# The opening of a two-layer diffusion backbone in two-chunk steps, with the context moved between latent features and their products

## The chip, the cores and the metric

One core of a Trainium2 chip runs the whole program. The metric is the device time of one execution in microseconds (us), the median of several.

## What is computed

The input is a latent stream `x` and a context stream `ctx`, each 256 tokens of 1024 features, and two conditioning vectors. Each of two layers mixes tokens by four branches and then applies a feed-forward block. The change concerns only the start of layer 0, up to the products q, k and v of the first branch:

```
mod = silu(c) @ w_mod[0] + b_mod[0]        # same with c_ctx for the context
sh1, sc1, ... = split(mod, 6)
h_lat = rmsnorm(x, norm_g[0, 0]) * (1 + sc1) + sh1
h_ctx = rmsnorm(ctx, norm_g[0, 0]) * (1 + csc1) + csh1
q, k, v = (h @ w_in[0])[..., :256], [256:512], [512:768]     # both streams
q, k = rope(q * 0.125), rope(k)            # the latent ones only
```

Everything else of `h @ w_in[0]`, the branches, the output projection, the feed-forward block and layer 1 follows and is the same code before and after.

## The kernel before

**Layout.** Features lie on partitions: a hidden state is 8 chunks of 128 features by 512 tokens (256 latent, then 256 context), kept as a hi and a lo tile in fp32r (`h0hi`, `h0lo`). Weights come as blocks of 128x1024 float32 (0.5 MB), by SP's queue, into four raw buffers (two tags of two). A block for a product is split into a hi tile (ACT, L102) and a lo tile (DVE, L112); a product is three matmuls, hi x hi, hi x lo, lo x hi (`mm3`, L205). A block of conditioning weights is used raw, as it lands.

**Who sets the order.** The program is a list of `Step`s, written out by hand in `begin` (L1288) for the opening. Ahead of each step `Weights.pump` (L114) loads as many of the opening's blocks as find a raw buffer whose former block is split (or, for conditioning, used), and splits what the step needs; then the step's code is issued. Each engine works its own instructions in that order, and SP issues its loads in that order, waiting for the buffer of each.

**The opening.** `x` is loaded, its squares are summed on ACT (`square`), the inverse root of the mean comes from POOL, DVE scales it (`x_norm`, L1301), PE turns it so that features lie on partitions (`x_turn`, tile `x0t`), DVE copies it to `x0s`. Meanwhile the conditioning product runs: one block is one chunk of 128 input features by 1024 outputs, shift and scale of four of the eight chunks of features, and `mod_mm` (L256) multiplies it in two matmuls of 512 columns. Its two results go to two strips of 32 of the array's columns (the two streams' conditioning vectors are the 32-column stationary operand `cs`). After eight blocks, a half, ACT copies the result to `modrows` (L1342), PE turns it (`modt`, L278), DVE adds the biases and makes `am` and `sh` (L283 to L286). Then `modulate` (L451) makes the hidden features of the half: `hf = x * am + sh`, one chunk on DVE and one on ACT, hi on ACT (L466), lo on DVE (L449).

The first half's products follow: v for two token tiles, then k, q, for the latent stream, with `v_part` (L1058) and `qk_part` (L1067), four chunks each, into banks of PSUM that `clear` (L1039) has filled with zeros. The eight blocks of the second conditioning half are multiplied between the products of the first half, with the context's features and products in between. Then the second half is turned to features (`late`, L1379), and its products follow, v of the latent stream first. After the context's v the values are centred on DVE (L678, L679); after k and q `rotate` (L714) applies the rope table, on ACT and DVE. The rope table and other constants are loaded by `fixed` (L649). The opening ends with the first matmul of the gate projection (`gps`); `retention` (L747) then starts beside it, its first products being `ktp` and, from `kt` and `vd`, `st` (L775).

Of the kernel before, what the change touches and what calls it, by code (L numbers as in the profile page):

```python
# [17 lines left out]
P = 128  # L18
# [14 lines left out]
MOD_ORDER = (0, 2, 1, 3)  # L33
# [4 lines left out]
WARM = (3,)  # L38
# [22 lines left out]
class Weights:  # L61
# [76 lines left out]

    def split_to(self, nth):
# [17 lines left out]
def kernel(ctx: ExitStack, tc: tile.TileContext, a: dict, out: bass.AP):  # L157
# [46 lines left out]

    def mm3(ps, st, mv, first, last):  # L205
# [38 lines left out]
    chan = load(cst, [P, DEPTH, 2, 4], a["chan"], "chan", nc.scalar)  # L244
    bsel = load(cst, [P, 2], a["c_bsel"], "bsel", nc.scalar)
    e12 = load(dec, [P, 2, 2 * PIECE], a["c_e12"], "e12", nc.scalar)
    kexp = load(dec, [P, 2, 2], a["c_kexp"], "kexp", nc.scalar)
# [8 lines left out]
    def mod_mm(k, half, raw):  # L256
        if "ps" not in mods:
            mods["ps"] = bank("m", "modps")
        ps = mods["ps"]
        for j in range(2):  # L260
            q = 2 * half + j
            nc.tensor.matmul(
                ps[32 * q : 32 * q + 32, :],
                lhsT=cs[:, k, :],
                rhs=raw[:, j * 512 : (j + 1) * 512],
                start=(k == 0),
                stop=(k == KC - 1),
            )
# [4 lines left out]
    def mod_cols(half, tiles, rows):  # L273

        pt = bank("b", f"modt{half}", [4, 64])
        hs = slice(64 * half, 64 * half + 64)
        for cb in range(4):
            nc.tensor.transpose(pt[:, cb, :], rows[hs, cb * P : (cb + 1) * P], ident[hs, hs])  # L278
        am, sh = tiles
        ks = slice(4 * half, 4 * half + 4)  # L280
        for s in range(2):
            b = [bcol[:, 0, kind, ks] for kind in range(2)]
            nc.vector.tensor_tensor(sh[:, s, ks], pt[:, :, s], b[0], op=ALU.add)  # L283
            nc.vector.tensor_tensor(am[:, s, ks], pt[:, :, 32 + s], b[1], op=ALU.add)
            nc.vector.scalar_tensor_tensor(
                am[:, s, ks], am[:, s, ks], 1.0, gcol[:, 0, 0, ks], op0=ALU.add, op1=ALU.mult  # L286
            )
# [325 lines left out]
    def mixer(l, h, hnext, start=None):  # L613
# [422 lines left out]
        if l == 0:  # L1036
            vps, kps, qps = {}, {}, {}

            def clear():  # L1039
# [4 lines left out]
                yield  # L1044
                for i in range(2):
                    vps[i], kps[i] = bank("a", f"vps{i}", [2, MIX]), bank("a", f"kps{i}")
                for n in (0, *WARM):
                    for i in range(2):
                        for ps in (vps[i].rearrange("p a b -> p (a b)"), kps[i]):
# [516 lines left out]
```

## Time and profile before

| | |
|---|---|
| time, median of 3 runs | 1244.37 us (1244.19 to 1245.08) |
| time of the profiled execution | 1246.01 us |
| its span, first to last instruction | 1244.2 us |
| PE busy | 1205.8 us, 97% of the span |
| DVE busy | 776.5 us, 62% |
| ACT busy | 452.4 us, 36% |
| POOL busy | 41.2 us, 3% |
| moved by DMA | 206.29 MB, mean 166 GB/s |
| chain of work that ended last, share of PE | 89% |

PE is the tensor engine, DVE the vector engine, ACT the scalar engine, POOL the general one; SP issues loads. Busy times are sums over instructions; a busy PE is not PE at its peak, since matmuls are pipelined and each record is longer than its share of the pace. Start times count from the first instruction of the span.

### The profile page before, as it was taken

Reading aid. Unit: us, or ns where it says so; the run is one execution under the profiler, and the core shown is the slowest. Engines: PE = TensorE matmul, PEld = TensorE weight load, DVE = VectorE, ACT = ScalarE, POOL = GpSimd, SP = SyncE. Lnnn points to the kernel's source line nnn. Section 1 sums busy time; section 2 is a strip of 40 time slices with the busy share of each in tenths; the row PEclk is TensorE's granted clock in tenths of the full one; section 3 lists DMA queues with packets and bytes.
Section 4 is the critical chain, followed back from the end, with each engine's and each line's share of the span. In section 5 each row is a group of like instructions: output and inputs, shape, how many; then the busy total and the mean of one; then the engine's idle time right before and its main releaser. Section 6 shows DMA issues by size and latency. Waiting matters only on the chain.

```text
span 1244.2 us, 17237 instructions
## 1 busy us (share of the span) xinstructions
PE 1205.8 (97%) x6790; PEld 1032.6 (83%) x6790; DVE 776.5 (62%) x1242; ACT 452.4 (36%) x712; POOL 41.2 (3%) x39
## 2 busy tenths in 40 slices
PE   6999999999999989999999999989999999999997
PEld 2687878888888788888888888779889998999986
DVE  4454464477887465776777674475666666666644
ACT  3332332323322453222222222354335445444532
POOL 1500000000000000000000000000000000000000
PEclk9999999999999989999999999999999999999999
DMA  8542323546755224666756783343455563656662
GB/s 291 180 130 84 102 85 107 209 151 168 203 176 190 82 94 126 225 209 158 246 185 205 226 270 105 112 134 136 123 153 183 178 225 116 201 176 185 196 220 88
DMA packets 66433, 206.29 MB, mean 166 GB/s; under 512 B 14640, under 2 KB 18224, under 8 KB 66352
## 3 DMA queue, kind: packets, MB, share of 16 engines
q1 hardware_dynamic: 65200, 204.96, 52.8%
q8 instruction: 53, 0.87, 0.3%
q10 hardware_dynamic: 1152, 0.24, 0.1%
q14 instruction: 28, 0.23, 0.1%
HBM read 204.06 MB, written 1.11 MB: 165 GB/s over the span
## 4 chain that ended last, share of the span: by engine, by line
PE 89%; DVE 4%; ACT 3%; issue 1%; DMA 1%; POOL 0%; SPq 0%; DVEq 0%; POOLq 0%; ACTq 0%
PE up L208 10%; PE up L209 10%; PE up L207 10%; PE gate L207 7%; PE gate L209 7%; PE gate L208 7%; PE dn L209 4%; PE dn L208 4%; PE dn L207 4%; PE pb L209 2%; PE pb L207 2%; PE pb L208 2%; PE wo L209 1%; PE wo L207 1%; PE wo L208 1%
## 5 line engine op out<-in xcount | busy, mean ns | idle before, releaser
L317 DVE SCALAR_TENSOR_TENSOR mjunk<-raw_mod,crow 128x1024 bf16<-128x1024 f32 x128 | 156.4, 1222 | 11.1 <-DMA raw_mod<-in_w_modt 8.9
L208 PE MATMUL up<-hm0lo,hi_up 128*128 128x512 f32 (+1 forms) x384 | 143.6, 374 | 0.5 <-DVE hm0lo L449 0.5
L207 PE MATMUL up<-hm0hi,hi_up 128*128 128x512 f32 (+1 forms) x384 | 143.8, 375 | 0.0
L209 PE MATMUL up<-hm0hi,lo_up 128*128 128x512 f32 (+1 forms) x384 | 143.7, 374 | 0.0
L112 DVE TENSOR_TENSOR lo_up<-raw_up,hi_up 128x1024 fp32r<-128x1024 f32 x88 | 107.5, 1223 | 36.2 <-ACT hi_up L102 36.2
L112 DVE TENSOR_TENSOR lo_gt<-raw_gt,hi_gt 128x1280 fp32r<-128x1280 f32 x64 | 95.3, 1489 | 30.5 <-ACT hi_gt L102 30.2
L207 PE MATMUL gate<-h0hi,hi_gt 128*128 128x512 f32 x256 | 100.5, 392 | 0.0
L207 PE MATMUL up<-hm1hi,hi_up 128*128 128x256 f32 x352 | 100.3, 285 | 0.0
L208 PE MATMUL up<-hm1lo,hi_up 128*128 128x256 f32 x352 | 100.3, 285 | 0.0
L209 PE MATMUL up<-hm1hi,lo_up 128*128 128x256 f32 x352 | 100.1, 284 | 0.0
L209 PE MATMUL gate<-h0hi,lo_gt 128*128 128x512 f32 x256 | 99.6, 389 | 0.0
L208 PE MATMUL gate<-h0lo,hi_gt 128*128 128x512 f32 x256 | 99.6, 389 | 0.0
L102 ACT ACTIVATE hi_up<-raw_up 128x1024 fp32r<-128x1024 f32 x88 | 92.1, 1048 | 7.2 <-DMA raw_up<-in_w_up 6.6
L102 ACT ACTIVATE hi_gt<-raw_gt 128x1280 fp32r<-128x1280 f32 x64 | 81.0, 1266 | 28.0 <-DMA raw_gt<-in_w_gate 28.0
L112 DVE TENSOR_TENSOR lo_dn<-raw_dn,hi_dn 128x1024 fp32r<-128x1024 f32 x44 | 53.6, 1224 | 51.4 <-ACT hi_dn L102 51.2
L988 ACT ACTIVATE sg<-gate 128x512 f32<-128x512 f32 (+1 forms) x64 | 31.3, 490 | 148.1 <-PE gate L209 146.8
L208 PEld LDWEIGHTS up<-hm0lo,hi_up 128*128 128x128 f32 x384 | 73.4, 191 | 13.1 <-DVE hm0lo L449 0.7
L207 PEld LDWEIGHTS up<-hm0hi,hi_up 128*128 128x128 f32 x384 | 73.5, 191 | 12.6
L209 PEld LDWEIGHTS up<-hm0hi,lo_up 128*128 128x128 f32 x384 | 73.3, 191 | 12.4
L102 ACT ACTIVATE hi_dn<-raw_dn 128x1024 fp32r<-128x1024 f32 x44 | 46.4, 1058 | 91.8 <-PE dn L209 67.1
L207 PE MATMUL gate<-hf0hi,hi_gt 128*128 128x256 f32 x256 | 73.4, 287 | 0.0
L209 PE MATMUL gate<-hf0hi,lo_gt 128*128 128x256 f32 x256 | 72.4, 283 | 0.0
(327 smaller groups left out, 2759.7 us busy)
## 6 DMA issues: line engine op xcount, KB each, us to landing
raw_up<-in_w_up SPq DMA_DIRECT2D x88, 512.0 KB, 3.9
raw_gt<-in_w_gate SPq DMA_DIRECT2D x64, 640.0 KB, 4.0
raw_mod<-in_w_modt SPq DMA_DIRECT2D x80, 512.0 KB, 4.1
raw_dn<-in_w_down SPq DMA_DIRECT2D x44, 512.0 KB, 4.3
raw_in<-in_w_in SPq DMA_DIRECT2D x28, 512.0 KB, 3.7
raw_mod<-in_w_mod SPq DMA_DIRECT2D x16, 512.0 KB, 4.5
raw_wo<-in_w_o SPq DMA_DIRECT2D x16, 512.0 KB, 4.2
grow<-gscr SPq DMA_DIRECT2D x6, 512.0 KB, 7.4
```

The source lines that it names most:

```text
L102: self.nc.scalar.activation(b.hi, b.raw, AF.Copy)
L112: self.nc.vector.tensor_tensor(b.lo, b.raw, b.hi.bitcast(F32), op=ALU.subtract)
L207: nc.tensor.matmul(ps, lhsT=st[0], rhs=mv[0], start=first, stop=False)
L208: nc.tensor.matmul(ps, lhsT=st[0], rhs=mv[1], start=False, stop=False)
L209: nc.tensor.matmul(ps, lhsT=st[1], rhs=mv[0], start=False, stop=last)
L317: nc.vector.scalar_tensor_tensor(junk, b.raw, 1.0, crow[s], op0=ALU.mult, op1=ALU.mult, accum_out=out()[:, s, i : i + 1])
L988: nc.scalar.activation(sg, ps, AF.Sigmoid)
```

## The change

The opening now goes by quarters, two chunks of features each, instead of halves.

- A conditioning block is now shift and scale of two chunks for two chunks of input; `mod_mm` multiplies it in eight matmuls of 128 columns, in four strips of 32 of the array's columns. Four blocks make a quarter, so sixteen blocks as before. `mod_cols` turns a quarter in one transpose and makes `am` and `sh` in three DVE operations.
- The first four blocks go to buffers of the ring of split tiles (`raw0`), not to raw buffers; `Weights.fetch` asks for the first v block, and for k and q, at set places. Four constants (`load_late`) go from ACT's queue at the start to SP's queue after the first quarter.
- Of the squares and the scaling of x, one token tile in two is done on DVE and the other on ACT. Three of the four latent transposes are done between the first four blocks, the fourth after the first v part.
- In each quarter the latent v part comes first, then the context's features are made, then k and q of the latent stream, then two conditioning blocks of the next quarter, the context's v, two more blocks, one k part, the next quarter's latent features, and the rest of k and q. Parts take two chunks (`v_part` both token tiles at once), with the products that need the lo tiles last.
- Weights are split in places of their own (`split_of`), as soon as the ring of split tiles has room. `WARM` sets how many zero fills of PSUM stand in which place: eight now come first of all.

The core of the diff:

```diff
-WARM = (3,)
+WARM = (2, 0.5, 0, 1)
...
+    def fetch(self, n):
+
+        for _ in range(n):
+            assert self._load(self.first[0])
...
-    chan = load(cst, [P, DEPTH, 2, 4], a["chan"], "chan", nc.scalar)
...
+    def load_late():
+        for t, src in ((e12, "c_e12"), (kexp, "c_kexp"), (chan, "chan"), (bsel, "c_bsel")):
+            nc.sync.dma_start(t, a[src])
...
-    def mod_mm(k, half, raw):
+    def mod_mm(quarter, pair, raw):
...
+        ps = mods["ps"][:, quarter * P : (quarter + 1) * P]
+        for i in range(2):
+            k = 2 * pair + i
+            for q in range(4):
+                nc.tensor.matmul(
+                    ps[32 * q : 32 * q + 32, :],
+                    lhsT=cs[:, k, :],
+                    rhs=raw[:, (4 * i + q) * P : (4 * i + q + 1) * P],
+                    start=(k == 0),
+                    stop=(k == KC - 1),
+                )
...
+        first_step(0, opening, lambda: x_norm((0, 1)))
+        first_step(1, partial(lat_turn, "v"), partial(lat_turn, "a"))
+        first_step(2, partial(lat_turn, "v"))
+        split_of(vb[0])
+        first_step(3, opening)
+        add(lambda: cols(0), opening, lambda: hidden(0, 0))
+        V_(0, 0)
+        add(lambda: x_norm((2, 3), lambda: (lat_turn("v"), weights.split_to(kb[0].nth))))
         for c in range(2):
             K_(0, c, 0)
...
+        split_of(qb[0])
+        add(lambda: hidden(1, 0))
+        for c in range(2):
+            Q_(0, c, 0)
+        for q in range(4):
+            if q:
+                V_(q, 0)
+                add(lambda q=q: hidden(1, q))
+                for fn in (K_, Q_):
+                    for c in range(2):
+                        fn(q, c, 0)
...
+            if q == 3:
+                add(fixed)
+            for j in range(2):
+                if q < 3:
+                    mod_step(q + 1, j, *([more] if q < 2 else []))
+            V_(q, 1)
+            for j in range(2, 4):
+                if q < 3:
+                    mod_step(q + 1, j, *([more] if q == 0 and j == 2 else []))
+            K_(q, 0, 1)
+            if q < 3:
+                add(lambda q=q: (cols(q + 1), hidden(0, q + 1)))
...
```

How the order moves, at three places. On SP, from the first load of x on, before (`x` is latent up to `x_176`):

```order
L1299 DMA x_176<-in_x 128x512
L94 DMA raw_mod_193<-in_w_mod 128x1024
L94 DMA raw_mod_195<-in_w_mod 128x1024
L94 DMA raw_mod_197<-in_w_mod 128x1024
L94 DMA raw_mod_199<-in_w_mod 128x1024
L94 DMA raw_mod_226<-in_w_mod 128x1024
L94 DMA raw_mod_230<-in_w_mod 128x1024
L94 DMA raw_mod_248<-in_w_mod 128x1024
L94 DMA raw_mod_259<-in_w_mod 128x1024
L94 DMA raw_v_277<-in_w_v 128x1024
```

and now:

```order
L1326 DMA x_176<-in_x 128x512
L1431 DMA mod_128<-in_w_mod 128x1024
L1431 DMA mod_129<-in_w_mod 128x1024
L1431 DMA mod_130<-in_w_mod 128x1024
L93 DMA raw_v_208<-in_w_v 128x1024
L1431 DMA mod_131<-in_w_mod 128x1024
L1326 DMA x_211<-in_ctx 128x512
L1326 DMA x_212<-in_ctx 128x512
L1326 DMA x_215<-in_ctx 128x512
L1326 DMA x_216<-in_ctx 128x512
L93 DMA raw_k_219<-in_w_k 128x1024
L93 DMA raw_q_221<-in_w_q 128x1024
```

Four conditioning blocks instead of eight stand ahead of the first products' data, and the context and k follow them at once.

On PE, at the end of the second quarter of the new opening (quarter 1; `vps_186` is the context's v, `kps_185` and `kps_187` are k, `modt` is the turned conditioning of quarter 2):

```order
L217 MATMUL qps_313<-h0hi_113,lo_q_392 128x256
L283 MATMUL modps<-raw_mod_452,cs 32x128 x8
L283 MATMUL modps<-raw_mod_479,cs 32x128 x8
L1087 MATMUL vps_186<-hi_v_295,h0hi_112 128x256
...
L1087 MATMUL vps_186<-lo_v_296,h0hi_113 128x256
L283 MATMUL modps<-raw_mod_491,cs 32x128 x8
L283 MATMUL modps<-raw_mod_520,cs 32x128 x8
L217 MATMUL kps_185<-h0hi_112,hi_k_369 128x256
...
L298 MATMUL modt_664<-ident,modrows 128x128
L217 MATMUL kps_187<-h0hi_112,hi_k_369 128x256
```

Conditioning blocks, which stood one by one between products, now stand in pairs, and a k part stands between a quarter's last block and its transpose.

On SP around the rope table, before:

```order
L94 DMA raw_in_594<-in_w_in 128x1024
L94 DMA raw_in_647<-in_w_in 128x1024
L198 DMA rope_741<-in_c_rope 128x512
L198 DMA fcs_743<-in_c_fd 128x256
L198 DMA fcn_745<-in_c_fn 128x1024
```

and now:

```order
L93 DMA raw_in_764<-in_w_in 128x1024
L93 DMA raw_in_794<-in_w_in 128x1024
L93 DMA raw_in_878<-in_w_in 128x1024
L206 DMA rope_904<-in_c_rope 128x512
L206 DMA fcs_906<-in_c_fd 128x256
```

The rope table now stands behind a third weight block, whose raw buffer is that of `raw_in_764`.

## Rows read from the trace of the kernel before

**Rows 1.** Spans and granted clock (core: span, mean granted clock).

```profile
core 0: 1244.2 us, clock 0.994
```

**Rows 2.** Busy time by stretch: engines with (x instructions), granted clock, DMA share, GB/s.

```profile
0.00:5.00 5.00, 0.00 (x0) 0.00 (x0) 1.68 (x9) 1.50 (x2) 0.20 (x4) 1.00 0.56 153
5.00:10.00 5.00, 0.07 (x2) 0.10 (x4) 0.00 (x0) 1.20 (x3) 3.23 (x1) 1.00 0.92 310
25.00:30.00 5.00, 4.96 (x33) 3.76 (x32) 4.55 (x10) 4.93 (x12) 0.00 (x0) 1.00 1.00 381
...
9.90:77.30 67.40, 63.62 (x411) 43.81 (x412) 35.59 (x99) 23.90 (x50) 18.96 (x6) 1.00 0.63 214
```

**Rows 3.** Timeline of PE, 0 to 75 us: start, length, operation [idle before <-releaser].

```profile
9.94 3.63 PE L262 MATMUL modps<-raw_mod,cs 128*32 128x512 f32 x8 [9.94 <-DMA raw_mod<-in_w_mod]
...
16.29 1.05 PE L262 MATMUL modps<-raw_mod,cs 128*32 128x512 f32 x4
...
26.79 0.47 PE L207 MATMUL vps<-hi_v,h0hi 128*128 128x256 f32 x1
...
49.91 1.91 PE L262 MATMUL modps<-raw_mod,cs 128*32 128x512 f32 x8
...
56.60 0.39 PE L207 MATMUL vps<-hi_v,h0hi 128*128 128x256 f32 x1 [1.15 <-ACT h0hi L466]
...
58.74 0.60 PE L1319 MATMUL x0t<-ident,x 128*128 128x128 f32 x4
...
62.41 0.66 PE L1319 MATMUL x0t<-ident,x 128*128 128x128 f32 x4 [1.63 <-ACT hf L460]
```

**Rows 4.** Timeline of PE, 60 to 95 us.

```profile
77.29 0.40 PE L207 MATMUL gps<-h0hi,hi_in 128*128 128x512 f32 x1
...
88.55 0.66 PE L775 MATMUL st<-vd,kt 128*64 128x128 f32 x8
89.13 0.50 PE L207 MATMUL fu<-h0hi,hi_in 128*128 128x512 f32 x1
```

**Rows 5.** Timeline of PE, 16.28 to 16.30 us: what starts by then.

```profile
16.29 0.62 PE L262 MATMUL modps<-raw_mod,cs 128*32 128x512 f32 x2
```

**Rows 6.** Timeline of PE, 134.60 to 134.62 us: what starts by then.

```profile
134.60 0.38 PE L866 MATMUL fa<-fcs,fu 128*128 128x256 f32 x1
```

**Rows 7.** Timeline of ACT, 0 to 80 us.

```profile
23.34 0.59 ACT L1342 ACTIVATE modrows<-modps 64x512 f32<-64x512 f32 x1 [11.58 <-PE modps L262]
24.37 1.06 ACT L102 ACTIVATE hi_v<-raw_v 128x1024 fp32r<-128x1024 f32 x1 [0.44 <-DMA raw_v<-in_w_v]
25.33 0.58 ACT L460 ACTIVATE hf<-x0s,sh,am 128x256 f32<-128x256 f32 x1
25.82 0.70 ACT L466 ACTIVATE h0hi<-hf 128x256 fp32r<-128x256 f32 x2
```

**Rows 8.** Timeline of DVE, 0 to 97 us.

```profile
24.48 0.16 DVE L283 TENSOR_TENSOR sh<-modt,bcol 128x4 f32<-128x4 f32 x1 [0.81 <-PE modt L278]
...
25.16 0.41 DVE L462 TENSOR_SCALAR hf<-x0s,am,sh 128x256 f32<-128x256 f32 x1
...
77.77 0.44 DVE L724 STREAM_SHUFFLE roper<-roper 128x256 f32<-128x256 f32 x1
...
79.94 0.45 DVE L724 STREAM_SHUFFLE roper<-roper 128x256 f32<-128x256 f32 x1
...
83.66 1.22 DVE L112 TENSOR_TENSOR lo_in<-raw_in,hi_in 128x1024 fp32r<-128x1024 f32 x1
...
85.39 0.89 DVE L764 TENSOR_TENSOR vd<-v,kdec 128x128 f32<-128x128 f32 x4
```

**Rows 9.** Timeline of SP's queue, 0 to 100 us.

```profile
60.57 0.43 SPq L198 DMA_DIRECT2D rope<-in_c_rope  x1
```

**Rows 10.** The tile `rope`: from its load's issue to landing.

```profile
DMA to landing us min/median/max: 3.8/3.9/4.0
```

**Rows 11.** Timeline of POOL, 0 to 90 us.

```profile
47.44 10.94 POOL L412 TENSOR_TENSOR dv<-two,dy 128x66 f32<-128x66 f32 x1
```

More of the change, by code (lines that the diff above doesn't have):

```diff
@@ L137, in pump @@
             self.flush()
+    def fetch(self, n):
+        for _ in range(n):
+            assert self._load(self.first[0])
+            if self.first.pop(0).split:
+                self.loaded += 1
+            else:
+                self.read += 1
     def split_to(self, nth):
@@ L203, in split, with mm3s @@
         nc.vector.tensor_tensor(lo, src, hi.bitcast(F32), op=ALU.subtract)
+    def mm3s(todo, last):
+        for n, (i, j) in enumerate(((0, 0), (0, 1), (1, 0))):
+            for m, (ps, st, mv) in enumerate(todo):
+                nc.tensor.matmul(ps, lhsT=st[i], rhs=mv[j], start=False, stop=last and n == 2 and m == len(todo) - 1)
     def mm3(ps, st, mv, first, last):
@@ L254 @@
     gscr = dram.tile([DEPTH, 2, 2, D], F32, name="gscr")
-    def mod_mm(k, half, raw):
+    def mod_mm(quarter, pair, raw):
         if "ps" not in mods:
             mods["ps"] = bank("m", "modps")
[L259 to L268, printed above, removed]
+        ps = mods["ps"][:, quarter * P : (quarter + 1) * P]
[9 more added lines that the diff above has]
+                )
+        return ps
@@ L1053, in clear @@
[L1053 to L1063 removed]
+                ends = [x for i in range(2) for x in (vps[i].rearrange("p a b -> p (a b)"), kps[i])]
@@ L1288, in begin @@
     def begin(rt, ot, v_part, qk_part, fixed, clear):
-        xn, xt, ready, steps = {}, [], [], []
+        xn, xt, steps = {}, [], []
         tiles = mod_tiles(0, 0)
         decay = decays()
+        rows = {}
         def x_load(t, new):
@@ L1352, in part, with mod_step @@
-        def part(fn, half, b, free, *args):
-            add(partial(fn, b, half, *args), blocks=[b], free=[b] if free else [])
+        def mod_step(quarter, pair, *fns):
+            b = Block(a["w_mod"][quarter, pair], f"mod00{quarter}{pair}", split=False)
+            add(partial(mod_part, quarter, pair, b), *fns, blocks=[b])
         vb = [Block(a["w_v"][0, i], f"v0{i}") for i in range(2)]
@@ new lines, in loads @@
+        def loads():
+            first_load(3)
+            ctx_load()
+            weights.fetch(2)
+        add(begin_loads, opening, more)
+        steps[-1].ahead = -1
+        steps.append(Step([], lambda: weights.fetch(1), tick=False, ahead=-1))
+        steps.append(Step([], loads, tick=False, ahead=-1))
+        first_step(0, opening, lambda: x_norm((0, 1)))
+        first_step(1, partial(lat_turn, "v"), partial(lat_turn, "a"))
+        first_step(2, partial(lat_turn, "v"))
+        split_of(vb[0])
```

262 lines of the change are left out of this document (124 added, 138 removed).

## Prediction

> **What bounds the kernel now.** I read the page first: PE is busy 97% of the span, so time is won by giving PE less to do or by filling its holes. The change touches only the opening (steps ahead of the first gate projection); from there on the order of every engine is the same. So I read PE's timeline for that stretch. PE sees its first matmul at 9.94, when the first conditioning block lands; the first v product starts at 26.79 and the opening ends at 77.29, with the first gps matmul [rows 3, 4]. From 9.9 to 77.3 PE is busy 63.62 of 67.40 us [rows 2]: what holes there are after the start are two waits for modulated features, 1.15 us at 56.60 and 1.63 us at 62.41 [rows 3]. The opening is thus a late start, 16.9 us in which PE does conditioning and transposes only, and 50.5 us of nearly full PE.
>
> A difference of 0.2%, 2.5 us, is about what a measurement of this kernel can tell from no change.
>
> **Step 1, the first v product comes earlier.** Before, all eight blocks of the first conditioning half must land, be multiplied and be copied out ahead of it; now four blocks (two chunks of features) do. Bytes ahead of the fourth one: x 4 x 0.262 MB, four blocks of 0.524 MB, one v block asked for in between, and about 0.16 MB of constants, 3.8 MB. The queues moved 153 and 310 GB/s in the first two 5-us windows, 2.3 MB by 10 us [rows 2]. The other 1.5 MB take 4.9 us at 310 GB/s or 4.0 us at the 381 GB/s of the fullest window. Landing lags the bytes: x, the first block and the constants, some 1.75 MB, had been moved at about 8.2 us, and PE got the block at 9.94, 1.7 us later. So the fourth block lands between 15.7 and 16.6; I take 16.0.
>
> Its product then costs a block of the new form. Of the old form a block is 1.05 us, two adjoining ones 1.91 us [rows 3], so 0.86 us of array time each. Two records start together there (x2 at 16.29), while a product over the whole array starts one at a time (x1 at 134.60) [rows 5, 6]: two column groups run side by side. The new form cuts the same work into 128 columns in four groups. Four side by side halve the array time, to 0.43 us a block; only two, and it stays 0.86 us. That is the unknown price; no row has four groups. The nearest row is st, 128 columns in two groups: 8 records in 0.58 us from 88.55 to the next matmul [rows 4], as fast as two groups allow, so at 128 columns nothing else is in the way yet. I take four, 0.55 us for a block standing alone.
>
> From there to the first v product it was about 3.5 us (23.3 to 26.79). Now: copying the rows out, 0.59 us for 512 columns [rows 7], about 0.3 for 128; one transpose 0.3 instead of four; three DVE operations instead of the six that took from 24.48 to 25.16 [rows 8], 0.35; hf on ACT 0.58 and the first of two h0hi, half of 0.70 [rows 7]; hand-overs 0.2: 2.1 us. So 16.0 + 0.55 + 2.1 = 18.65 instead of 26.79, **8.1 us earlier**. The squares, now half on DVE and half on ACT, and the three transposes lie in the shadow of those landings. If that cover were gone, the 4 us from squares to x0s would be late, not the landing.
>
> **Step 2, from the first v product to the end: 50.5 us before.** The 288 products of q, k and v stay. Removed: seven places with conditioning blocks (six of 1.05 us, one pair of 1.91 us, 8.2 us). Added: twelve blocks in six adjoining pairs, each 1.91 - 0.86 = 1.05 us with four groups, 6.3 us: **-1.9 us**. One latent transpose group moves in, 0.60 us with its tail, 0.4 of it at PE's pace [rows 3]: **+0.4 us**. Small transposes of conditioning (+3) and zero fills of q's banks (-2) I set to nothing. The two old waits go, **-2.8 us**: context work of at least 2.9 us of k and q products now stands between latent features and their users, and the splits stand a quarter ahead of their use.
>
> New waits come in the first quarter. Behind the fourth conditioning block the queue still owes the context (1.05 MB) and the k and q blocks: k is complete at 5.4 MB, 3.1 MB past the 10-us mark; at the middle of 310 and 381 GB/s that is 19.0, landed 20.7. Its hi split takes ACT 1.06 us, to 21.8, its lo split DVE 1.22 us, to 23.05 [rows 7, 8]. PE has done the v part and a transpose group by 20.75, waits 1.05 us for hi, does four products and waits 0.75 us for lo; q's lo split, third in DVE's row behind the two x scalings, costs 0.25 us more, and the fourth block of the next quarter, whose buffer q's split frees, up to 0.4 us: **+2.4 us**. Without them it is 0; with k at 310 GB/s 4. Later quarters take some 11.7 us of PE each and ask for five or six blocks of 0.524 MB, 225 to 270 GB/s, under the 310 shown, and each is asked for a half quarter ahead: 0, at most 1 us each.
>
> 50.5 - 1.9 + 0.4 - 2.8 + 2.4 = 48.6: the opening ends at 18.65 + 48.6 = 67.3 instead of 77.29.
>
> **Step 3, what is late next.** The rope table is fetched from SP's queue, now behind a third weight block, which waits for the first lo split of the next weights. That split ends some 3.1 us ahead of the end of the opening; the rope load is issued 0.5 us later and takes 3.9 us [rows 9, 10]. So DVE's first rotation, which needs it, stops until 1.4 us past the end. Then, from there: 1.1 us for its rest, a lo split of 1.22, three rotations at the pace of 77.77 to 79.94, 2.17 us, less 0.6 for the copies ahead of the first, and a lo split with g and vd, 2.6 us from 83.66 to 86.28 [rows 8]: vd ends 12.2 us past the end. PE asks for it at st, 88.55 - 77.29 = 11.3 us past the end; before, vd was ready at 86.28, with 2.3 us to spare. With the hand-over **+1.1 us**; below 0 is excluded, since st stands in a fixed place; 3 if the load takes 6.
>
> The four constants that move to SP's queue cost four issues of some 0.43 us there, beside loads that wait for buffers anyway. The long power on POOL (10.94 us before, done at 58.4) starts by about 46 and is needed by about 70 [rows 11]: nothing.
>
> **Sum.** -8.1 (step 1) - 1.9 + 0.4 - 2.8 + 2.4 + 1.1 = **-8.9 us**. The profiled execution took 1246.01 us (span 1244.2) and would take 1237.1; the median of the three runs, 1244.37, is 1.6 us below it, so **1235.5 us**. Its own range: 1233 to 1238.5.
>
> **Rivals.**
> *Two groups at a time.* If four column groups don't run side by side, each of six pairs costs 0.86 us more and the last of the first four blocks 0.43: 5.6 us, of which some 0.6 falls into the waits of the first quarter: 1240.5. For it: the trace shows never more than two. Against it: st's pace. The Trainium skill (TensorE: Matmul & The Clock Gate, "Wait — 56ns, not 53.3ns?") gives 62 ns a MATMUL as a bound of the sequencer when decoding is not done in hardware; on a block's 16 records that would be 1.0 us, this rival's time, on its 8 instructions 0.5 us, the forecast's. By that rule, st's 8 records would take 0.50 us; the 0.58 us of the trace agrees and so doesn't settle it.
> *Late data.* x, conditioning, v, context and k now all stand in one queue; if the fourth block lands at 19 rather than 16, all but the slack behind it is late: 1238.5.
> *Given back behind the opening.* The rotation chain of step 3 is 3 us later than I reckon (fcn, inv and the weights share its queue): 1238.5.
> *The clock, slower than before.* The first eight conditioning records took 3.63 us, the same number later 1.91 us [rows 3]: they ran at 1.2 GHz, not 2.4. The mean granted clock of 0.994 says the same: 0.6% of 1244 us, doubled, is 15 us at half clock, the time up to the first dense stretch [rows 1]; the clock column of the windows reads 1.00 there all the same [rows 2], so I go by the records. Now eight zero fills run from 4 us on, but from 7.5 to 18.6 PE works in short pieces between landings. If the clock then stays low, each microsecond of full-speed work costs one more; from 9 us of such work on the gain is gone, and with 13 us it is 1248. Against it: in the trace dense work brought the clock up after some 5 us, which costs at most 2.5 us here, most of it in waits for k that are there anyway.
>
> **Chances.** Forecast 0.62, two groups 0.18, late data 0.09, given back 0.07, clock 0.04. Forecast and the three middle cases are all over 2.5 us faster: faster 0.94; same 0.03 and slower 0.03 share the clock's case, with its milder end and a mishap of the others. The range 1232 to 1241 takes in the forecast's bounds (no first-quarter waits: -2.4; no rope wait: -1.1) and the three cases above it, and leaves out the clock's and the tails.
>
> **What would show it.** In the new trace: first v product near 18.6; conditioning pairs in later quarters 1.05 us long, with four records starting together; waits of some 2 us for k's splits between 20 and 25, none over 1 us from 33 to 67; first gps near 67; a DVE wait for rope, and a PE wait of about 1 us at st. I am wrong if the pairs last 1.9 us, if the first v starts past 21, if matmuls past 24 us run at half their present pace, or if the gain at gps is not there at the end of the span.

## The result and the profile after

The changed kernel takes 1238.35 us (median of five, 1237.05 to 1239.95) where the kernel before, in five runs beside it, takes 1245.08: a ratio of 0.9948, 95% interval 0.9934 to 0.9963, or 6.7 us faster. The forecast was 1235.5 with a range of 1232 to 1241. In a second set of runs, on another occasion, the same two kernels gave 1236.06 against 1244.32, a ratio of 0.9935 (0.9922 to 0.9947), 8.3 us faster.

| | before | after |
|---|---|---|
| profiled execution, us | 1246.01 | 1237.05 |
| its span, us | 1244.2 | 1235.3 |
| PE busy, us | 1205.8 | 1199.7 |
| first v product, us | 26.79 | 16.83 |
| opening ends (first `gps` matmul), us | 77.29 | 63.90 |
| `st`, us | 88.55 | 79.25 |

The spans differ by 8.9 us, exactly the forecast's sum. That is partly luck: as the last lines of the table show, the opening ends 13.4 us earlier, and 4.1 us of that is lost again in the 15 us behind it.

The start, in the timeline of PE from 0 to 30 us, columns as in [rows 3]:

```profile
3.98 0.61 PE L1067 MATMUL vps<-zero 128*128 128x512 bf16 x1 [3.98 <-DVE zero L1063]
...
8.83 0.65 PE L283 MATMUL modps<-mod,cs 128*32 128x128 f32 x16 [1.28 <-DMA mod<-in_w_mod]
9.41 0.39 PE L1067 MATMUL vps<-zero 128*128 128x512 bf16 x1
...
14.00 0.65 PE L283 MATMUL modps<-mod,cs 128*32 128x128 f32 x16 [1.03 <-DMA mod<-in_w_mod]
...
16.83 0.93 PE L1087 MATMUL vps<-hi_v,h0hi 128*128 128x256 f32 x4 [0.60 <-ACT h0hi L486]
...
19.45 0.51 PE L217 MATMUL kps<-h0hi,hi_k 128*128 128x256 f32 x2 [0.29 <-ACT hi_k L101]
...
21.07 0.51 PE L217 MATMUL kps<-h0hi,lo_k 128*128 128x256 f32 x2 [0.88 <-DVE lo_k L111]
...
24.43 1.08 PE L283 MATMUL modps<-raw_mod,cs 128*32 128x128 f32 x32
25.44 0.74 PE L1087 MATMUL vps<-hi_v,h0hi 128*128 128x256 f32 x4
```

These answer to [rows 3]. The fourth conditioning block is there at 14.00, the first v product follows at 16.83. A block alone occupies PE for 0.58 us (8.83 to 9.41), an adjoining pair for 1.01 us (24.43 to 25.44). The waits for k's splits, 0.29 and 0.88 us, are there but short.

Whether four column groups run side by side is read as in [rows 5]: the same timeline, cut to 24.42 to 24.54 us, counts the records that have started by then.

```profile
24.43 0.32 PE L283 MATMUL modps<-raw_mod,cs 128*32 128x128 f32 x4
```

Four have started within 0.03 us of the first; [rows 5] had two.

What feeds the start is in the table by stretches (columns as in [rows 2], stretches of 5 us):

```profile
5.00:10.00 5.00, 3.72 (x25) 1.09 (x22) 2.25 (x9) 1.83 (x6) 4.24 (x3) 1.00 1.00 357
10.00:15.00 5.00, 3.84 (x63) 2.52 (x62) 3.09 (x5) 2.36 (x4) 0.00 (x0) 1.00 1.03 408
```

The queues move 357 and 408 GB/s; before it was 310 in the first of these stretches, and 381 in its fullest one [rows 2].

The end of the opening, PE's timeline from 62 to 82 us, answers to [rows 4]:

```profile
63.90 0.40 PE L221 MATMUL gps<-h0hi,hi_in 128*128 128x512 f32 x1
...
71.98 0.58 PE L221 MATMUL gps<-h0hi,hi_in 128*128 128x512 f32 x1 [2.23 <-ACT q L743]
72.36 0.63 PE L222 MATMUL gps<-h0lo,hi_in 128*128 128x512 f32 x1
...
75.73 0.39 PE L221 MATMUL gps<-h0hi,hi_in 128*128 128x512 f32 x1
```

and from 60 to 96 us:

```profile
79.25 0.66 PE L795 MATMUL st<-vd,kt 128*64 128x128 f32 x8
79.83 0.50 PE L221 MATMUL fu<-h0hi,hi_in 128*128 128x512 f32 x1
```

Here is the new wait. The second gate projection (the `gps` at 71.98) writes the PSUM bank that held the first q product, and waits 2.23 us until ScalarE has copied q out. Behind it nine matmuls stand 0.43 us apart where those at 63.90 and at 75.73 stand 0.23 apart: PE runs at half its clock, which costs another 1.7 us. `st` itself does not wait, 15.35 us behind the end of the opening where it was 11.26 before [rows 4].

Why q's copy is late is told by three more timelines (DVE, ACT, and SP's queue, which answers to [rows 9]):

```profile
67.32 0.69 DVE L745 TENSOR_TENSOR roper<-roper,rope 128x512 f32<-128x512 f32 x1 [3.63 <-DMA rope<-in_c_rope]
...
77.14 0.89 DVE L784 TENSOR_TENSOR vd<-v,kdec 128x128 f32<-128x128 f32 x4
```

```profile
71.27 0.38 ACT L741 ACTIVATE roper<-qps 128x256 f32<-128x256 f32 x1 [2.02 <-DVE k L746]
71.55 0.38 ACT L743 ACTIVATE q<-qps 128x256 f32<-128x256 f32 x1
```

```profile
62.15 0.43 SPq L206 DMA_DIRECT2D rope<-in_c_rope  x1
```

The rope table is asked for at 62.15, only 1.75 us ahead of the end of the opening, and DVE's first rotation stands 3.63 us for it. The four rotations share one buffer (`rr`), so ScalarE may not begin on q until k's second rotation is done (the 2.02 us at 71.27), and its copy releases the bank only then.

**A loss that is not the change's.** Mean granted clock times span is what the span would be at full clock, and the rest is what half clock costs. For the kernel before, 37 runs on three chips give 1236.9 us and 5.8 us; for the changed kernel ten runs in two sets give 1228.1 and 7.4. At full clock the change is thus worth 8.8 us, and about 1.6 us more go to the clock, 6 to 11 us in a single run. These figures are good to about a microsecond: the clock is given to three digits, one of which is 1.2 us, and in the two profiles 2.0 us (before) and 1.3 us (after) of what they count lie behind PE's last matmul, where half clock costs nothing. Where it goes is seen in the granted clock (the column with 1.00 or less) of stretches of 10 us, of before:

```profile
440.00:450.00 10.00, 6.99 (x55) 6.50 (x54) 7.62 (x15) 5.72 (x15) 2.91 (x4) 0.92 0.09 36
450.00:460.00 10.00, 9.35 (x57) 8.75 (x56) 5.31 (x13) 4.67 (x12) 0.00 (x0) 0.74 0.45 159
...
1040.00:1050.00 10.00, 8.09 (x60) 6.46 (x59) 7.47 (x15) 5.51 (x15) 1.64 (x3) 0.95 0.35 107
1050.00:1060.00 10.00, 10.00 (x76) 10.00 (x76) 6.83 (x14) 6.16 (x12) 0.00 (x0) 0.88 0.27 75
```

and of after:

```profile
70.00:80.00 10.00, 8.02 (x33) 6.15 (x34) 7.92 (x18) 4.61 (x10) 0.00 (x0) 0.83 0.41 116
...
440.00:450.00 10.00, 8.75 (x58) 8.01 (x59) 5.95 (x14) 4.67 (x12) 0.00 (x0) 0.83 0.44 158
...
820.00:830.00 10.00, 7.19 (x48) 6.66 (x47) 7.09 (x13) 5.73 (x11) 0.54 (x1) 0.84 0.19 66
830.00:840.00 10.00, 10.00 (x71) 9.90 (x70) 5.88 (x11) 6.16 (x13) 0.00 (x0) 0.83 0.66 222
```

A stretch of 10 us at 0.83 has lost 1.7 us. The 70 to 80 of after is the wait for q's bank. The others lie at or behind stretches in which PE had been waiting for VectorE or ScalarE (6.99 of 10 us busy, 7.19 of 10), in code that the change leaves as it was. Which of them are hit differs from run to run: from 20 us to the last matmul every fall of the clock lost 1.7 us, or twice that in one piece, three times in all in the profile of before, four times in that of after, and two to five times in the profiles of the experiments. That is a part of the spread of the times.

### The profile page after: what moved, and what is told of

Same layout as the page of the kernel before. It is cut to its first block, busy times and chain, and to the rows that moved or that the text cites. A ratio compares the mean times of both kernels' runs of the same rounds, so it can differ in the third digit from the quotient of the medians.

```text
span 1235.3 us, 17599 instructions
## 1 busy us (share of the span) xinstructions
PE 1199.7 (97%) x6976; PEld 1037.2 (84%) x6976; DVE 778.1 (63%) x1245; ACT 452.5 (37%) x711; POOL 40.8 (3%) x39
## 4 chain that ended last, share of the span: by engine, by line
PE 87%; DVE 5%; ACT 3%; DMA 2%; issue 1%; POOL 1%; SPq 0%; DVEq 0%; POOLq 0%; ACTq 0%
PE up L223 10%; PE up L222 10%; PE up L221 10%; PE gate L221 7%; PE gate L222 7%; PE gate L223 7%; PE dn L223 4%; PE dn L222 4%; PE dn L221 4%; PE pb L222 2%; PE pb L223 2%; PE pb L221 2%; PE wo L222 1%; PE wo L221 1%; PE wo L223 1%
```

## The experiments

The theory: the opening did what was reckoned; the loss behind it comes from the rope table alone, through the one rotation buffer and q's bank. The rivals: the rotation chain is late for its own work; the clock falls with or without a wait; whatever is gained is given back further on. Times are compared by their ratio to the kernel before, run beside them; these runs are from three chips (the first four kernels on one, the next four on another, the two repeats and the last two on a third), on which the kernel before takes 1244.3 to 1244.5 us. The numbers "at full clock" are means of span times granted clock.

**The changed kernel again.** No edit.

> The changed kernel itself once more, beside the others on one chip. Expected 1238 us, 6 to 7 us under the kernel before, with PE's wait for the second gate projection (near 72 us) again some 2 us and the matmuls behind it 0.43 us apart for some 3.5 us. If the few us between its runs come from the clock behind that wait, the stretch of half pace will differ in length between the two profiles while everything ahead of 64 us agrees within 0.3 us.

Measured: 1236.06 us (1235.85 to 1237.68). First v product 18.09, end of the opening 64.89, a wait of 2.22 us at 72.96, `st` at 78.75. So the wait is there to a hundredth, but this time the matmuls behind it stand 0.23 us apart: the clock did not fall. The two profiles do not agree within 0.3 us ahead of 64 us, as they should have; the first v product differs by 1.26 us, of which the last experiments tell more.

**The rope table a quarter earlier.**

```diff
-            if q == 3:
+            if q == 2:
                 add(fixed)
```

> Theory (late rope table): PE's 2.23 us at the second gate projection hangs on the rotation chain, which started 3.63 us late for the table. With the table asked for a quarter earlier, q's copy out of its bank comes near 68 us, ahead of the 69.7 at which PE asks for the bank: the wait goes, with it the nine matmuls at half pace (1.75 us): 4.0 us under the changed kernel, 1234.3 us, st near 75.3 and no DVE wait for rope. Rival A (the chain is as late for its own work: lo splits and rotations on DVE, the copies on ACT): the wait keeps over 1 us, gain at most 1.2 us. Rival B (the clock falls here with or without a wait): the wait goes, the half pace stays, gain 2.2 us. Rival C (what the opening gains is given back further on, whatever st does): st 4 us earlier, the end of the span less than 1 us earlier.

Measured: 1234.31 us (1231.91 to 1238.24), ratio 0.9923 (0.9907 to 0.9939); repeated on another occasion (`e1_again`, below) 1233.06 (1232.60 to 1235.23), 0.9914 (0.9899 to 0.9928). PE's timeline behind the opening:

```profile
76.02 0.66 PE L795 MATMUL st<-vd,kt 128*64 128x128 f32 x8
```

No wait at the second gate projection, no wait of DVE for rope, no half pace, and `st` 11.25 us behind the end of the opening (64.77), as in the kernel before [rows 4]. The theory holds, rivals A and B fall. (`fixed` loads a few other constants behind the rope table, and the edit moves them too; DVE's wait was for the table.) The start of the products moves by up to 2.6 us from profile to profile, so the distance from the first v product to `st` says more than the time of `st`: 62.42 and 60.66 us in the two profiles of the changed kernel, 58.58 here and 58.38 in the repeat. The 2.1 to 4.0 us between them are the wait of 2.2 and, in the first profile, the half clock of 1.7 behind it. Of these, some 1.5 to 3 us arrive at the end (1226.7 at full clock in ten runs, 1.4 less than the changed kernel). One place where time is lost again is seen in the second layer. PE's timeline there, of this kernel:

```profile
912.62 2.42 PE L832 MATMUL y<-am,v 128*64 128x256 f32 x8 [2.19 <-DVE am L818]
```

and of the changed kernel's second and first profile:

```profile
912.90 1.68 PE L832 MATMUL y<-am,v 128*64 128x256 f32 x8 [0.87 <-DVE am L818]
```

```profile
914.14 1.68 PE L832 MATMUL y<-am,v 128*64 128x256 f32 x8 [1.44 <-DVE am L818]
```

DVE stands there for small loads of decay rows (`qd`), 5.25 us against 3.94 in the second profile, so PE comes 1.6 us earlier than there and leaves only 0.3 us earlier; behind the wait the clock falls (2.42 us for the eight records instead of 1.68). That would be rival C in part. But the two profiles of the changed kernel differ here by 0.57 us as well, so how much of it belongs to the edit is not shown.

**The rope table late, two rotation buffers.**

```diff
-            raw = rt("rr", [2, SEQ], "roper")
+            raw = rt("rr", [2, SEQ], "roper", 2 if l == 0 else 1)
...
-                z = rt("rr", [SEQ], "zero").bitcast(BF16)
+                z = rt("rr", [SEQ], "zero", 2).bitcast(BF16)
```

> The rope table stays late; layer 0's rotations get a second buffer, so that q's copy out of the bank need not wait for k's second rotation. Theory (late table, handed on through the one buffer): q's copy comes one rotation earlier, near 69.3 us, PE's wait at the second gate projection falls from 2.2 to about 0, but the end of the chain (vd near 78.0) does not move, and PE asks for it at st some 4 us earlier, near 75.3: the wait goes to st, about 2.5 us long. Gain 0 to 1.8 us, the upper end if the half pace does not come back behind st. Rival (the bank alone sets the price, the chain behind it has time): gain 4 us, no wait at st.

Measured: 1236.40 us (1233.14 to 1239.65), 0.9934 (0.9917 to 0.9951). PE's timeline:

```profile
77.20 0.75 PE L795 MATMUL st<-vd,kt 128*64 128x128 f32 x8 [1.19 <-DVE vd L784]
```

With DVE's wait for rope still 3.48 us long, q's copy comes at 69.53 and PE's wait at the bank is gone. It stands at `st` instead, for `vd`, 1.19 us. That is the wait the prediction had put there; the changed kernel does not reach it, since the bank stops PE first. That its size too is near the forecast's 1.1 us is chance: the table lands 3.3 us behind the end of the opening and not 1.4, and the second buffer takes 1.2 us off the chain. The wait is shorter than the 2.5 us expected here, because the second buffer also takes some of the chain's length away (rope's landing to `vd`'s end 9.5 us, in the changed kernel 10.7). The median does not tell this kernel from the changed one; at full clock its four runs give 1226.3 us, 1.8 less than the changed kernel and as much as with the early table, which is the upper end of the theory's 0 to 1.8.

**Context behind k and q,** and then the same with the early rope table. This prices the place of the context's features. It is not quite the order of the kernel before, which made them between k and q in its first half and between the v parts in its second.

```diff
             if q:
                 V_(q, 0)
-                add(lambda q=q: hidden(1, q))
                 for fn in (K_, Q_):
...
+            if q:
+                add(lambda q=q: hidden(1, q))
             if q == 3:
                 add(fixed)
```

> One part of the change undone: the context's modulated features are again made behind the products of k and q of the latent quarter, not ahead of them. Theory: the two waits for modulated features that the kernel before had in its later quarters (1.15 and 1.63 us) come back, and the opening ends 2.5 to 3.5 us later, near 67 us; 2.5 to 3.5 us slower than the changed kernel, 1241 us. In the first quarter it may help, since the k and q splits are waited for there: then PE's waits for the splits grow instead, by up to 2 us. Rival: the splits a quarter ahead are enough by themselves, no wait over 0.5 us appears in the quarters 1 to 3, and the time is that of the changed kernel within 1 us.

Measured: 1237.20 us (1236.71 to 1237.58), 0.9940 (0.9928 to 0.9953): no difference from the changed kernel. PE's timeline:

```profile
38.80 0.92 PE L1087 MATMUL vps<-hi_v,h0hi 128*128 128x256 f32 x4 [0.53 <-ACT h0hi L486]
...
51.34 0.93 PE L1087 MATMUL vps<-hi_v,h0hi 128*128 128x256 f32 x4 [0.53 <-ACT h0hi L486]
...
63.71 0.93 PE L1087 MATMUL vps<-hi_v,h0hi 128*128 128x256 f32 x4 [1.54 <-ACT h0hi L486]
...
68.32 0.40 PE L221 MATMUL gps<-h0hi,hi_in 128*128 128x512 f32 x1
...
79.58 0.66 PE L795 MATMUL st<-vd,kt 128*64 128x128 f32 x8
```

Waits for modulated features are back (0.53 us twice and 1.54; [rows 3] had 1.15 and 1.63), now all for the context's v, and the opening ends 3.4 us later than the changed kernel's 64.89. The time is nevertheless the same, and not because the waits stayed away, as the rival said: the rope table, asked for at 62.10 as ever, is now early enough, the bank does not stop PE, and `st` stands about where it stood. What the context's place wins, the late table takes. If so, the fourth corner should gain nothing.

> Both edits at once: context features behind k and q (as in e5) and the rope table a quarter earlier (as in e1). With e0, e1 and e5 that makes four corners. Theory (what the context's place gains was swallowed by the late table): in e5 the second gate projection did not wait, st stood at 79.6 us as in e0, though the opening ended 3.4 us later. So here nothing is left for the early table to win: the opening ends near 68.3, st near 79.5, 1237 us, as e5, while the context's place is worth some 3 us at st where the table is early (e1: 76.0). Rival (the table's gain and the context's gain add up): st near 76.5, 1234.5 us.

Measured: 1236.84 us (1235.83 to 1238.13), 0.9938 (0.9922 to 0.9954); opening ends 67.43, `st` 78.68. The four corners: the distance from the first v product to `st` in the profiles (with the context behind, that product stands at 18.02 and 17.12), then the time at full clock:

| | context ahead of k, q | context behind |
|---|---|---|
| rope late | 62.42, 60.66; 1228.1 | 61.56; 1228.0 |
| rope early | 58.58, 58.38; 1226.7 | 61.56; 1228.9 |

The early table alone gives nothing at `st`, the context's place alone between 0.9 us lost and 0.9 us won, both together 3.0 to 3.2. At the end of the span the pair with the table late is equal, the pair with it early differs by 2.2 us. The gains do not add; each needs the other.

**Splits later,** on the kernel with the early table.

```diff
-                split_of(vb[1])
-            if q == 1:
-                split_of(kb[1])
...
-            if q == 1:
-                split_of(qb[1])
```

> On e1 (rope table early): the second halves of the weights of v, k and q are split about half a quarter to a quarter later and, with that, asked for behind one to four more conditioning blocks. Theory (the early splits are a margin, not a gain, since PE waited for none of them in quarters 1 to 3): no wait over 0.5 us between 33 us and the end of the opening, st near 76, time within 1.5 us of e1. Rival (the early splits carry part of step 2): waits for splits or for conditioning blocks of 1 to 3 us in quarters 1 and 2, st at 77 to 79.

Measured: 1239.92 us (1238.36 to 1241.56), 0.9961 (0.9948 to 0.9975), some 5 us above the kernel it was made from. I was wrong here, and the rival right and still too mild. PE's timeline from 20 to 72 us:

```profile
44.40 0.74 PE L1087 MATMUL vps<-hi_v,h0hi 128*128 128x256 f32 x4 [0.57 <-ACT hi_v L101]
...
49.63 0.51 PE L217 MATMUL kps<-h0hi,hi_k 128*128 128x256 f32 x2 [2.79 <-ACT hi_k L101]
...
50.89 0.79 PE L217 MATMUL kps<-h0hi,lo_k 128*128 128x256 f32 x2 [0.42 <-DVE lo_k L111]
```

and the stretch of 10 us around it:

```profile
50.00:60.00 10.00, 9.58 (x114) 8.62 (x113) 2.49 (x6) 0.93 (x3) 4.39 (x1) 0.83 0.79 243
```

Three waits of 3.8 us together, and the clock falls behind the 2.79 us for k (0.83, 1.7 us): 5.5 of the 5.6 us by which the opening is longer (52.93 us from the first v product to its end at 70.69, against 47.33). Early splits are thus no margin: that no wait was seen was their doing.

**Transposes late.** Only one latent transpose group ahead of the first v product; the kernel before had all four there, so this prices the place, not the change.

```diff
-        first_step(1, partial(lat_turn, "v"), partial(lat_turn, "a"))
-        first_step(2, partial(lat_turn, "v"))
+        first_step(1, partial(lat_turn, "v"))
+        first_step(2)
...
-        add(lambda: x_norm((2, 3), lambda: (lat_turn("v"), weights.split_to(kb[0].nth))))
+        add(lambda: x_norm((2, 3), lambda: weights.split_to(kb[0].nth)))
...
-                add(lambda q=q: (cols(q + 1), hidden(0, q + 1)))
+                add(lambda q=q: (lat_turn("v"), cols(q + 1), hidden(0, q + 1)))
```

> One part undone on the changed kernel with the late rope table: only one latent transpose group ahead of the first v product; the other three are made in the quarters that use them, each with its copy out of PSUM ahead of the modulated features. Two of them leave PE's idle start and enter the dense part: two times 0.4 to 0.6 us at PE's pace, so the opening 0.8 to 1.2 us longer; the third only moves within the dense part. The copies and the features made from them lie beside PE's products, no wait. If the late table swallows it as it swallowed the context's place, st and the end move by less than 0.5 us. Rival: transposes and features now stand one behind the other, 1 us and more of waiting in each of three quarters, opening 3 to 4 us longer.

Measured: 1245.67 us (nine runs of 1241.90 to 1247.98), 1.0007 (0.9996 to 1.0018): all of the gain is gone. The same kernel once more:

> The kernel of e8 once more, since its time (1246 us in nine runs) was far above both theories and its one profile came from a stretch in which the whole chip ran several times slower and showed nothing usable but the order of the waits: PE waited three times 0.9 us for the copy of a late transpose group ahead of the transpose of the conditioning rows. Theory 1 (three waits of 0.9 us, and behind each a further wait for the features made from the copy): opening 4 to 5 us longer than the changed kernel's, st near 84, time 1242. Theory 2 (in addition, PE's start is emptier without the transposes, and the clock comes up later or falls again there): conditioning blocks, first v part and k part at the pace of half clock, some 3 us more, 1245. Theory 3 (it was the chip): 1239.

Measured: 1244.64 us (1241.84 to 1246.89), 1.0001 (0.9992 to 1.0011). PE's timeline:

```profile
30.55 0.30 PE L298 MATMUL modt<-ident,modrows 128*128 128x128 f32 x1 [0.88 <-DVE x0s L1377]
...
78.19 0.56 PE L221 MATMUL gps<-h0hi,hi_in 128*128 128x512 f32 x1 [4.02 <-ACT q L743]
```

and its stretch from 10 to 20 us:

```profile
10.00:20.00 10.00, 7.54 (x74) 4.79 (x75) 5.83 (x16) 5.31 (x12) 0.71 (x2) 0.83 1.04 409
```

The first v product is none the later (16.99), so theory 2 falls as a price. Its cause did come: the clock falls at 10.2 us and stays at half until 13.6, and the second and third conditioning block take 1.08 us each. They lie ahead of the landing of the fourth (14.16), for which PE waits anyway, so it costs nothing here. The 0.88 us stand three times, once a quarter, and the opening is 51.3 us long instead of 47.1. Then the wait at the second gate projection is 4.02 us instead of 2.23, though the rope table stands as late as before (asked for at 66.57, again 1.75 us ahead of the end of the opening at 68.32): it ends with ScalarE's copy of the second q (77.76), not of the first (75.60), so the other order has given that projection the other q's bank. The clock falls, and `st` stands at 85.46, 6.2 us later than in the changed kernel. At full clock the end is 5.7 us later (19 runs), and 9.2 us are lost to the clock instead of 7.4.

**Constants ahead of the squares,** on the kernel with the early table.

```diff
-    chan = cst.tile([P, DEPTH, 2, 4], F32, name="chan")
+    chan = load(cst, [P, DEPTH, 2, 4], a["chan"], "chan", nc.scalar)
...
-        for t, src in ((e12, "c_e12"), (kexp, "c_kexp"), (chan, "chan"), (bsel, "c_bsel")):
-            nc.sync.dma_start(t, a[src])
+        pass
```

(`bsel`, `e12` and `kexp` likewise.)

> One part undone, on e1: the four small constants are fetched again on ScalarE's queue at the start and not on SyncE's later. Their fetches held ScalarE's squares of x back from 4.5 to 8.8 us in the kernel before. Theory (x is not what the start waits for): the squares come some 4 us later, the transposes move from about 9 to 12 us, still ahead of the fourth conditioning block (landed at 14.0 in the changed kernel); first v product within 0.5 us, time within 1 us of e1. Rival (x is on the path): the first v product 2 to 4 us later, at 20 to 21, and the time with it.

Measured: 1235.94 us (1234.94 to 1237.48), 0.9929 (0.9912 to 0.9947); 1226.3 at full clock against 1226.7. The squares start at 8.46 instead of 3.96, yet the transposes only at 12.43, between the 11.76 and 12.63 of the two profiles of the kernel with the early table. The first v product stands at 19.20, within the expectation's half microsecond of one of the two profiles it is compared with (19.46 and 17.44) and 1.8 us from the other. Its first block came late too (9.44); from there it is 9.76 us, and 9.82 us in the later profile. No cost of the constants can be shown.

**The clock at the start.** The kernel with the early table once more, with four zero fills at its start instead of eight, and with ten.

```diff
-WARM = (2, 0.5, 0, 1)
+WARM = (1, 0, 0, 1)
```

```diff
-WARM = (2, 0.5, 0, 1)
+WARM = (2.5, 1, 0, 1)
```

> The early rope table once more, beside the others on this chip. 1234.3 us (1233 to 1236); st near 76; if the wait for y in the second layer (2.2 us there, 0.9 in e0) comes with the earlier start it is again about 2 us and some 1.3 us of the gain at st are lost there; if it was chance, about 1 us, and the end is 2.5 to 3 us ahead of the changed kernel.

> On e1: only the first four zero fills run at the start, PE then idles from about 5.7 us to the first conditioning block. Theory (the eight fills are what starts the rise of the clock): full pace comes later than the 13 us of e1, the conditioning blocks, the first v and k parts run at half pace (records twice as far apart) and the opening ends 1.5 to 4 us later. Rival (work ahead of the first block does nothing for the clock): first v product and opening within 0.5 us of e1.

> On e1: ten zero fills instead of eight at the start and four instead of two behind the first conditioning block, so that PE has fewer idle moments ahead of the features. In two of eight profiles so far the clock was up from 7 to 8 us on, and the first v product then came at 16.8 to 17.1 instead of 17.4 to 18.1. Theory (less idle time brings the clock up early more surely): first v product near 17.0, 0.5 to 1 us earlier than e1, 1233.5 us. Rival (when the rise comes is not in the kernel's hands): first v product as in e1 or 0.5 us later, since two more fills run behind the first block, 1234.5 to 1235 us.

Measured: 1233.06 us for the unchanged one, its wait for y 1.3 us in this profile, so the 2.2 us were in part chance; 1233.37 (three runs of 1233.29 to 1234.68), ratio 0.9916 (0.9899 to 0.9933), with four fills; 1233.27 (1232.58 to 1233.56) with ten, ratio 0.9911 (0.9896 to 0.9926). PE's timeline of the unchanged one:

```profile
9.64 1.08 PE L283 MATMUL modps<-mod,cs 128*32 128x128 f32 x16 [2.06 <-DMA mod<-in_w_mod]
...
19.46 0.93 PE L1087 MATMUL vps<-hi_v,h0hi 128*128 128x256 f32 x4 [1.04 <-ACT h0hi L486]
```

and with ten fills:

```profile
9.64 0.64 PE L283 MATMUL modps<-mod,cs 128*32 128x128 f32 x16 [1.21 <-DMA mod<-in_w_mod]
...
17.62 0.93 PE L1087 MATMUL vps<-hi_v,h0hi 128*128 128x256 f32 x4 [0.60 <-ACT h0hi L486]
```

Both have the first block at 9.64. With ten fills it takes 0.64 us, PE is at full clock from then on, and the first v product follows 7.98 us later; in the unchanged one it takes 1.08, at half clock, and the distance is 9.82 us. In twelve profiles of the changed kernel and its variants the distance is 8.0 us three times, with full clock from the first block on, 8.1 once (the late transposes above, whose first block is at full clock and whose next two are not), and 8.4 to 9.8 in the others. But four fills gave 9.0 us, in the middle of what eight gave, so the theory that eight fills start the rise has one profile against it and none for it. That ten make the early rise surer rests on one profile, and the times do not tell it from eight; it stays open.

## Why the prediction was right, and where it was not

The direction and the range were right. The sum of the profiled execution, -8.9 us, was met to 0.1 us because its errors cancelled:

- **Step 1, the first v product: 18.65 forecast, 16.83 measured** (16.99 to 19.46 in other profiles). The mechanism was right. Mis-sized was the landing of the fourth block, 16.0 forecast and 14.00 measured: I took 310 to 381 GB/s from stretches of the kernel before, and the new start draws 357, then 408. Why it draws more than the 381 is not shown: the DMA share was 1.00 there already, and it is 1.00 and 1.03 here. The Trainium skill (DMA: Bandwidth & Descriptors, "Where 436 GB/s comes from") puts loads from HBM at some 358 GB/s per core, half of what two cores share, and the fabric's ports at 435. Here one core runs, and the trace shows 408 and 406 GB/s in two stretches, so the first does not bind. From landing to first v product 2.83 us were measured against 2.65.
- **The four column groups (forecast 0.55 us a block and 1.05 a pair): 0.58 and 1.01.** Four records start together; the rival of two groups falls. By the rule that I had quoted from the Trainium skill (TensorE: Matmul & The Clock Gate), 62 ns for each of a pair's 16 instructions are 0.99 us, and four groups' array time is 0.86 us: between these the measured 1.01 us, hand-over included, does not decide. The starts within the pair do: its timeline, cut at 24.59, 24.81, 25.03 and 25.25, counts 8, 16, 24 and 32 records, so 24 records, two to an instruction, start in 0.66 us. That is 55 ns an instruction: the array's pace, and less than the rule's 62.
- **Step 2, the length from first v to the end of the opening: 48.6 forecast, 47.07 measured.** The waits of the first quarter were 1.7 us (0.29, 0.88, 0.24 for q, and 0.27 for the fourth block of the next quarter), not 2.4, since k too landed earlier; the pairs at 1.01 give 0.2 us more, and the rest of the 1.5 us stays open. The two old waits are gone, as forecast. Of the two reasons given, the context's place is worth 3.2 to 3.5 us of the opening (50.30 us with the context behind k and q, 47.07 and 46.80 with it ahead), and "the splits stand a quarter ahead" 5.5 us, each by taking it away; against the old order neither is measured.
- **Step 3, what is late next: +1.1 forecast, +4.1 measured** (+2.6 in the second profile). This is the step that failed. "The rope load is issued 0.5 us later and takes 3.9" was right in kind: the table landed 3.4 us behind the end of the opening rather than 1.4, as its issue stood 1.75 us ahead of that end (not 2.6) and its load took 5.1 us. But I followed the chain only to `vd` and `st`, and did not ask which PSUM bank the second gate projection takes, nor that the rotations share one buffer. The bank is asked for 5.9 us behind the end of the opening (71.98 less the wait), 5.4 us ahead of `st`; so a chain that is 2.0 us later than reckoned costs 2.23 us there and, in one profile of two, 1.7 us of half clock behind it. Even the forecast's own table, 1.4 us behind the end, would have had q's copy end 6.0 us behind it (it ends 4.6 us after the table lands: 71.93 less 67.32), just too late for the bank. "Below 0 is excluded, since st stands in a fixed place" looked at `st` alone, and the upper end of 3 was passed. Nearest was the rival "given back behind the opening", 0.07, which named the chain but not the bank.

Together: -1.8 (start), -1.5 (length), +3.0 (step 3), +0.4 further on, about 0 against the forecast.

**From the profile to the median** I carried over that the median lies 1.6 us below the profiled execution. For after it lies 1.3 us above. These 2.9 us are all that the forecast of 1235.5 is off. What they are is not shown. The granted clock does not explain them: the profiled run has 0.993 and the run at the median 0.995. The profile of after does have the earliest first v product of the twelve (16.83), and the half pace at the start is not in the granted clock.

**The clock's rival** was argued from a misreading. "15 us at half clock, the time up to the first dense stretch": the granted clock of 0.994 comes for the most part from stretches around 450 and 1050 us, as the rows above show (0.8, 2.6, 0.5 and 1.2 us lost in the four), and 2.0 us from the time behind the last matmul; the half pace at the start is not in it. By the pace of its matmuls the start ran at full clock from 7 to 9 us on at the earliest and from about 16 us on at the latest, so the rival did not come true.

The version that beats both is the changed kernel with the rope table a quarter earlier, 1233.1 to 1234.3 us: 0.9914 and 0.9923 of the kernel before; with ten fills 0.9911, which isn't told from it. The intervals of these ratios overlap with the changed kernel's 0.9922 to 0.9947; the 1.4 us at full clock and the missing wait speak for it.

## What to carry to other kernels

When a stage is made to end earlier, list every resource that the work behind it asks for, PSUM banks and single buffers as well as operands, with the time at which each comes free; the earliest one that is late sets the price, and a later wait for an operand is never reached. Loads that hang on the progress of something else in the same queue (here a constant behind a weight block that waits for a split) do not move with the stage: issue them where their own buffer allows. And judge an edit by the wait it removes together with the next one in line: counted from the first product, two edits that alone gave `st` nothing, or less than 1 us, gave it 3 us together.

## What was not expected of the hardware

- **A short hole in dense work may cost it twice.** Behind PE's waits of 2.23, 2.79 and 4.02 us the matmuls ran at half clock; behind a wait of 2.22 us in another execution of the same kernel, and behind 1.54 and 1.63 us, they did not. The length of the wait does not decide it: the clock also fell behind waits of 1.28 and 0.76 us (at 817 and 818 us, after) and of 1.91 us (at 1047, before), and not behind one of 2.62 (at 839, before). Each time it fell, the granted clock shows 1.7 us more, lost on top of the wait, or twice that.
- **The spread of the runs is in part the clock's.** Of two executions of one kernel the one at a mean granted clock of 0.992 took 1238.08 us and one at 0.997 took 1231.91; times their clocks, both spans are 1226.4 us. Over the ten runs of that kernel the standard deviation of the spans falls from 2.1 to 0.9 us when each is multiplied by its clock; over the 37 runs of the kernel before it does not fall (1.0 and 1.2).
- **The loads reached 408 GB/s** over 5 us where four conditioning blocks, the context and the first weights were asked for at once.
